# Differential attention in an 8-head, 1024-token layer: other banks and another order for projections, context weights and normalizing, and ScalarE in place of GpSimd for the high halves of copied parts

## The chip, the cores and the metric

The kernel runs on one core of a Trainium2 chip. A core has TensorE (PE in the profile; PEld are its weight loads), VectorE (DVE), ScalarE (ACT), GpSimd (POOL) and SyncE (SP), which here issues all transfers. Each engine works through its own list of instructions in order; semaphores hold an instruction until what it needs is there. PSUM, where TensorE puts its results, has eight banks of 512 fp32 columns. The metric is the device time of one execution in microseconds, the median of several. A single execution is also profiled, and all rows shown come from such an execution.

## The reference

Two layers over 1024 latent tokens and 256 context tokens of width 1024. Layer 0 mixes by differential attention and layer 1 by an S5 state-space layer; an MLP follows each. Only the attention of layer 0 is touched here:

```python
q_l = apply_rope(heads_qk(q_l), cos, sin) * scale      # 8 heads, 2 components of 64
k_l = apply_rope(heads_qk(k_l), cos, sin)
k_all = jnp.concatenate([k_c, k_l], axis=1)            # 256 context + 1024 latent keys
s = jnp.einsum('bqhcd,bkhcd->bhcqk', q, k)
p = jax.nn.softmax(s, axis=-1)
w = p[:, :, 0] - lam * p[:, :, 1]
o = jnp.einsum('bhqk,bkhe->bqhe', w, v)
o = rmsnorm(o, subln_g) * (1.0 - lambda_init)
```

Context queries see only context keys and have no rotary; latent queries see all 1280 keys. Everything is fp32.

## The kernel before

**Precision.** A product of two fp32 matrices is made of three matmuls (`mm3`, L132 to L134): each operand is split into a high half, which is a copy to fp32r (`split`, L137, on ScalarE), and a low half, the source minus the high half (L138, on VectorE or GpSimd).

**The stage.** Attention is the function `phase_b`. It goes through 8 heads with 9 units each, so 72 units `n`, and 5 more to finish. Unit 0 of a head holds the 256 context queries, units 1 to 8 hold 128 latent queries each. Queries are also counted in pairs of 256 (pair 0 is unit 0, pair 1 units 1 and 2, and so on). The loop writes the order of TensorE, VectorE, ScalarE and GpSimd out by hand (`manual`), and only SP's list is ordered by a scheduler.

A unit does the following, and the names are used from here on:

- *Scores* (L510, in unit 0 L504): two components, 2560 columns of PSUM, banks 0 to 4; in unit 0 banks 0 and 1 only.
- *Minima* (L523, L519 in unit 0): VectorE reads the scores (their sign is turned), writes them to SBUF and gathers the row minimum, once per component.
- *Exponentials* (L533, L530): ScalarE, one per component, with row sums.
- *Combination* (L541, L542, L544): VectorE makes the weights `w` of the unit.
- *Parts*: the weights of the unit before are transposed by TensorE (L556) in three parts of 4, 2 and 4 blocks of 128 columns, into bank 5, half of bank 6, and bank 7 or, if the unit has projection matmuls, bank 5 again. `w_evac` brings a part to SBUF as a high and a low half (`wT`). The first part goes directly: high on ScalarE (L564), low on VectorE (L565), both read PSUM. The others are *copied*: ScalarE copies the part to SBUF (L569), GpSimd makes high (L570) and low (L571) of the copy. Unit 0's weights have one part only, so unit 1 has one part to bring.
- *Values* (`values`): after each pair's second unit, in units 2 (pair 0, only 2 blocks), 4, 6, 8 and unit 1 of the next head, TensorE multiplies `wT` with the values into bank 6; they stand ahead of the transposes. In those units except for pair 0 the parts are brought to SBUF only after the combination. `pair_out` copies the result (L652), squares it on GpSimd (L653) and stores it to `od`.

**Projections of the next head.** Units 0, 2, 3, 5 and 7 make the queries and keys of head h+1 (`AHEAD`, `proj_group`): context keys and a first half of the latent keys in unit 0, the second half of the keys in unit 2, context queries in unit 3, the two halves of the latent queries in units 5 and 7. Every group is collected in bank 7 (the ring `qb`). The two groups of unit 0 differ: the first stands ahead of the scores and is brought out at once, the second is laid between the parts, as the groups of the other units are. A context group is brought out directly (L451, L452). A latent group goes through the rotary chain: `evac` at the end of its unit (L456, L457 and four transfers that swap rows), an empty step, `sine` on GpSimd (L462), `add` on VectorE (L465), `store` (a split, L137 and L138, and transfers to `Kd` or `Qd`). These steps lie in the list `post`; `next_post` takes one after the second part and one at the end of each unit. So the sine comes at the end of the next unit, the sum after the second part of the one after, and the store at its end.

**Normalizing of the head before.** In units 6, 7, 8, 0 and 1 one pair of the head before is normalized: `norm_load` at the start of the unit loads the pair from `od` and the factors from `rsd`; `norm_pair` at the end of the unit multiplies them (L684, VectorE), splits the product (high on ScalarE, L137 with 128x256 W<-W; low on GpSimd) and stores both to `on`. This starts in unit 6 of head 1, with head 0's result.

**Head 7** has no projections to make. In its units and the 5 that follow TensorE does the first part of the output projection (`wo_group`), and head 6's pairs are normalized by `norm6` and head 7's by `norm7`.

Of the kernel before, what the change touches and what calls it, by code (L numbers as in the profile page):

```python
# [70 lines left out]
class Prog:  # L71
# [359 lines left out]
    def proj_group(self, h, T, g, wt):  # L431
# [3 lines left out]
        b = self.qb.next()[:, 0:n]  # L435
# [35 lines left out]
        return [product(k) for k in range(8)], [direct] if g == 2 else [evac, None, sine, add, store]  # L471
# [89 lines left out]
    def w_evac(self, tb, hi, lo, direct):  # L561
        nc = self.nc
        if direct:
            nc.scalar.activation(hi, tb, AF.Copy)  # L564
            nc.vector.tensor_tensor(lo, tb, hi.bitcast(F32), ALU.subtract)  # L565
        else:
            m, n = tb.shape[1:]
            t = shaped(self.wraw.next()[:, 0 : m * n], (m, n))
            nc.scalar.activation(t, tb, AF.Copy)  # L569
            nc.gpsimd.tensor_scalar(hi, t, 1.0, 0.0, ALU.mult, ALU.add)  # L570
            nc.gpsimd.tensor_tensor(lo, t, hi.bitcast(F32), ALU.subtract)  # L571
# [8 lines left out]
    def b_start(self):  # L580
# [11 lines left out]
        for split, T in zip(splits, (1, 0)):  # L592
            split(0)
            wt = split(1)
            for g in (2, 0, 1):
                products, rest = self.proj_group(0, T, g, wt)
                for f in products:
                    f()
                for f in post:
                    f()  # L600
                rest[0]()
                post = rest[2:]
                yield
# [3 lines left out]
    def phase_b(self):  # L607
# [181 lines left out]
        ready = []  # L789
# [5 lines left out]
        with self.manual():  # L795
            for n in range(72 + 5):
# [6 lines left out]
                if front and n - 6 >= 9 and (n - 6) % 9 < 5 and (n - 6) // 9 < 7:  # L803
                    norm_load((n - 6) // 9 - 1, (n - 6) % 9)
                if h == 7 and u > 5:
                    load6(u)
                if front:
# [10 lines left out]
                    if h < 7:  # L818
                        groups = [self.proj_group(h + 1, *a, wts[a[0]]) for a in self.AHEAD.get(u, ())]
# [8 lines left out]
                    self.maxima(u, p, sm)  # L828
                if front:
# [12 lines left out]
                if pv:  # L842
                    values(*pv)
                for part in range(3):
                    if part < parts:
                        tb = pb[:, 256:512] if part == 1 else self.bank(7 if part == 2 and not groups else 5)
                        t = self.w_part(prev[1], prev[2], part, tb)
                        ready.append((*t, part == 0))
                    if not late or part == 2:
                        evac()  # L850
# [24 lines left out]
                next_post()  # L875
# [20 lines left out]
                if h < 8 and n - 6 >= 9 and (n - 6) % 9 < 5 and (n - 6) // 9 < 7:  # L896
                    norm_pair((n - 6) // 9 - 1, (n - 6) % 9)
# [1204 lines left out]
```

## Time and profile before

| | before |
|---|---|
| median of 3 runs | 3051.51 us (3049.69 to 3059.32) |
| profiled execution: time, span | 3048.01 us, 3046.2 us |
| granted clock of TensorE, mean | 0.978 |
| TensorE busy | 2855.1 us, 94% of the span |
| VectorE busy | 1909.6 us, 63% |
| ScalarE busy | 1256.1 us, 41% |
| GpSimd busy | 814.1 us, 27% |

The attention stage begins at about 238 us of the span and ends at about 905 us. In a row of a group of instructions the columns are: line, engine, operation, out<-in and shapes, count, then busy microseconds and mean nanoseconds of one, then the idle time of the engine just before them with what ended it. In a row in order of time they are: start, duration, engine, line, operation, and in brackets the idle time before it and what ended that. A row of waits has the total in microseconds, how often, and the longest.

### The profile page before, as it was taken

To read this page: it belongs to the slowest core of one execution; us is meant where nothing else is said; L and a number is where in the kernel's file an instruction comes from. 1 tells how busy PE (TensorE), PEld (TensorE's weight loads), DVE (VectorE), ACT (ScalarE), POOL (GpSimd) and SP (SyncE) were. 2 spreads that over 40 slices of the span, in tenths; PEclk is the share of its full clock that TensorE was granted. 3 is DMA by queue.
4 is the path that set the end of the run, shared out by engine and by line. 5 is a ranking of instruction groups with operands and counts; after the bars stand their busy time and mean duration, and the time that the engine had idled before them with its cause. 6 is when DMAs were issued, how large, how long until landed. Compare 5 with 4: busy or idle time off the path is not lost.

```text
span 3046.2 us, 42172 instructions
## 1 busy us (share of the span) xinstructions
PE 2855.1 (94%) x15376; PEld 2368.6 (78%) x15376; DVE 1909.6 (63%) x2766; ACT 1256.1 (41%) x2254; POOL 814.1 (27%) x794
## 2 busy tenths in 40 slices
PE   6998999999799999999999999688999899999998
PEld 4687888878687877788777778588787778888887
DVE  5357877777654654344677755899543666666555
ACT  3425555555544643333422222467344533222223
POOL 2314665666654400000100003566112200000003
PEclk9999999999899999999999999899999999999999
DMA  9955556556716455532666663577642221111113
GB/s 264 304 174 164 150 161 167 164 161 173 245 57 197 125 169 174 166 119 93 199 192 184 185 196 104 159 213 206 214 148 95 66 66 56 52 49 52 56 39 135
DMA packets 384235, 448.83 MB, mean 147 GB/s; under 512 B 54694, under 2 KB 299676, under 8 KB 382876
## 3 DMA queue, kind: packets, MB, share of 16 engines
q1 hardware_dynamic: 384028, 446.14, 49.1%
q8 instruction: 121, 1.98, 0.3%
q14 instruction: 86, 0.70, 0.1%
HBM read 320.88 MB, written 120.95 MB: 145 GB/s over the span
## 4 chain that ended last, share of the span: by engine, by line
PE 66%; DVE 10%; DMA 8%; issue 5%; ACT 4%; POOL 4%; SPq 3%; DVEq 0%; POOLq 0%; ACTq 0%
PE PS L132 19%; PE PS L134 19%; PE PS L133 19%; SPq L80 3%; PE PS L510 2%; ACT F L533 1%; PE PS L202 1%; DVE F L523 1%; DVE FD L1708 1%; PE PS L556 1%; PE PS L1690 1%; PE PS L1725 1%; DMA W<-rsd 1%; DVE FD L1699 1%; DVE R L138 1%
## 5 line engine op out<-in xcount | busy, mean ns | idle before, releaser
L132 PE MATMUL PS<-H,R 128*128 128x512 f32 (+1 forms) x960 | 361.3, 378 | 15.5 <-ACT F L569 13.8
L133 PE MATMUL PS<-H,R 128*128 128x512 f32 (+1 forms) x992 | 366.1, 369 | 2.9 <-POOL H L138 2.8
L134 PE MATMUL PS<-H,R 128*128 128x512 f32 (+1 forms) x960 | 348.9, 368 | 0.1
L133 PE MATMUL PS<-R,H 128*128 128x512 f32 x692 | 271.0, 392 | 0.0
L132 PE MATMUL PS<-R,H 128*128 128x512 f32 x676 | 268.2, 400 | 2.0 <-ACT R L137 1.6
L134 PE MATMUL PS<-R,H 128*128 128x512 f32 x676 | 260.1, 392 | 1.1 <-DVE H L138 1.1
L132 PE MATMUL PS<-R 128*128 128x256 f32 (+1 forms) x656 | 221.9, 339 | 7.0 <-ACT R L137 2.8
L132 PEld LDWEIGHTS PS<-H,R 128*128 128x128 f32 x960 | 184.3, 192 | 50.3 <-ACT F L569 15.2
L137 ACT ACTIVATE R<-W 128x512 fp32r<-128x512 f32 (+1 forms) x203 | 154.6, 766 | 161.1 <-PE PS L133 112.0
L1625 POOL TENSOR_SCALAR stat<-stat 128x1 f32<-128x1 f32 x24 | 14.9, 620 | 765.4 <-ACT PS L1623 765.1
L133 PE MATMUL PS<-R 128*128 128x256 f32 (+1 forms) x624 | 208.6, 334 | 9.1 <-DVE R L565 9.1
L1428 DVE TENSOR_TENSOR F<-PS,F 128x1024 f32<-128x1024 f32 (+1 forms) x113 | 136.4, 1212 | 128.3 <-PE PS L134 128.1
L133 PEld LDWEIGHTS PS<-H,R 128*128 128x128 f32 x992 | 191.4, 193 | 31.1 <-POOL H L138 3.6
L138 DVE TENSOR_TENSOR R<-W,R 128x512 fp32r<-128x512 f32 (+1 forms) x162 | 140.5, 872 | 114.5 <-ACT R L137 75.2
L134 PEld LDWEIGHTS PS<-H,R 128*128 128x128 f32 x960 | 184.3, 192 | 32.6 <-issue 2.1
L533 ACT ACTIVATE F<-F,stat 128x1280 f32<-128x1280 f32 x128 | 174.4, 1362 | 84.5 <-DVE F L523 84.2
L523 DVE TENSOR_SCALAR_CACHE_REDUCE F<-PS 128x1280 f32<-128x1280 f32 x128 | 185.1, 1483 | 8.6 <-PE PS L510 8.3
L570 POOL TENSOR_SCALAR R<-F 128x256 fp32r<-128x256 f32 (+1 forms) x128 | 124.2, 970 | 169.3 <-ACT F L569 147.5
L134 PE MATMUL PS<-R 128*128 128x512 f32 (+1 forms) x488 | 168.4, 354 | 0.0
L132 PE MATMUL PS<-H 128*128 128x512 f32 x408 | 161.0, 395 | 1.5 <-ACT H L137 1.5
L134 PE MATMUL PS<-H 128*128 128x512 f32 x408 | 159.4, 392 | 0.0
L510 PE MATMUL PS<-R,R 128*128 128x512 f32 x720 | 155.3, 364 | 0.4 <-DVE F L523 0.4
(426 smaller groups left out, 7037.8 us busy)
## 6 DMA issues: line engine op xcount, KB each, us to landing
W<-in_mlp_w SPq DMA_DIRECT2D x148, 256.0 KB
W<-in_mlp_w SPq DMA_DIRECT2D x68, 512.0 KB
FU<-in_ada_w SPq DMA_DIRECT2D x40, 512.0 KB
W<-in_ada_w SPq DMA_DIRECT2D x32, 512.0 KB
H<-hidd SPq DMA_DIRECT2D x64, 256.0 KB
W<-in_s_w_glu SPq DMA_DIRECT2D x64, 256.0 KB
hidd<-FU SPq DMA_DIRECT2D x52, 256.0 KB
recd<-FD SPq DMA_DIRECT2D x48, 256.0 KB
```

Of the source, the lines that this page charges most:

```text
L80: return self.nc.sync.dma_start(out=out, in_=in_)
L132: mm(out, ah, bh, start=first, stop=False, **kw)
L133: mm(out, ah, bl, start=False, stop=False, **kw)
L134: mm(out, al, bh, start=False, stop=last, **kw)
L137: self.nc.scalar.activation(hi, src, AF.Copy)
L138: (lo_eng or self.nc.vector).tensor_tensor(lo, src, hi.bitcast(F32), ALU.subtract)
L202: self.nc.tensor.matmul(acc[32 * j : 32 * j + 32, 0:256], self.scT[:, 2 * k : 2 * k + 32], w[:, 256 * j : 256 * j + 256], start=k == 0, st ...
L510: mm(self.PS[:, 1280 * c + k0 : 1280 * c + k1], Q[:, c, r, qs], K[c][:, k0:k1], start=r == 0, stop=r == 1)
L523: ts(p[c], self.PS[:, 1280 * c : 1280 * c + 1280], 1.0, None, ALU.mult, ALU.min, accum_out=sm[:, c : c + 1])
L533: nc.scalar.activation(p[c], p[c], AF.Exp, bias=sm[:, c : c + 1], scale=-1.0, accum_out=sn[:, 0:1] if c else s0[:, u + 1 : u + 2])
L570: nc.gpsimd.tensor_scalar(hi, t, 1.0, 0.0, ALU.mult, ALU.add)
L1428: nc.vector.tensor_tensor(acc[:, n : n + m], y[:, n : n + m], acc[:, n : n + m], ALU.add)
```

## The change

- The first of unit 0's two projection groups is collected in bank 4; all others stay in bank 7.
- The empty step of the rotary chain is dropped: the sine comes after the second part of the next unit, the sum one step later, the store after the second part of the unit after that.
- A new list `later` takes what used to be done at the end of a unit from `post`, and `norm_pair`. It is worked off in the next unit, right after the minima. `norm_load` comes behind it instead of at the unit's start.
- In units with values (except for pair 0) the first part is copied too, if the unit has three parts. If it has one (unit 1), its transposes stand ahead of the values, it goes directly, and it is brought out right away instead of after the combination.
- The high half of a copied part is made by ScalarE (still line L570) instead of GpSimd.

Units of all heads are affected alike; the stages before and behind are not edited.

```diff
-    def proj_group(self, h, T, g, wt):
+    def proj_group(self, h, T, g, wt, b=None):
...
-        b = self.qb.next()[:, 0:n]
+        b = (self.qb.next() if b is None else b)[:, 0:n]
...
-        return [product(k) for k in range(8)], [direct] if g == 2 else [evac, None, sine, add, store]
+        return [product(k) for k in range(8)], [direct] if g == 2 else [evac, sine, add, store]
...
             nc.scalar.activation(t, tb, AF.Copy)
-            nc.gpsimd.tensor_scalar(hi, t, 1.0, 0.0, ALU.mult, ALU.add)
+            nc.scalar.activation(hi, t, AF.Copy)
             nc.gpsimd.tensor_tensor(lo, t, hi.bitcast(F32), ALU.subtract)
...
-                post = rest[2:]
+                post = rest[1:]
...
-        ready = []
+        ready, later = [], []
...
-                if front and n - 6 >= 9 and (n - 6) % 9 < 5 and (n - 6) // 9 < 7:
-                    norm_load((n - 6) // 9 - 1, (n - 6) % 9)
...
-                        groups = [self.proj_group(h + 1, *a, wts[a[0]]) for a in self.AHEAD.get(u, ())]
+                        ahead = self.AHEAD.get(u, ())
+                        groups = [self.proj_group(h + 1, *a, wts[a[0]], self.bank(4) if a != ahead[-1] else None) for a in ahead]
...
                     self.maxima(u, p, sm)
+                while later:
+                    later.pop(0)()
+                if front and n - 6 >= 9 and (n - 6) % 9 < 5 and (n - 6) // 9 < 7:
+                    norm_load((n - 6) // 9 - 1, (n - 6) % 9)
...
-                if pv:
+                first = parts == 1
+                if pv and not first:
                     values(*pv)
                 for part in range(3):
                     if part < parts:
                         tb = pb[:, 256:512] if part == 1 else self.bank(7 if part == 2 and not groups else 5)
                         t = self.w_part(prev[1], prev[2], part, tb)
-                        ready.append((*t, part == 0))
-                    if not late or part == 2:
+                        ready.append((*t, part == 0 and (first or not late)))
+                    if pv and first and part == 0:
+                        values(*pv)
+                    if not late or first or part == 2:
                         evac()
...
-                next_post()
+                if post:
+                    later.append(post.pop(0))
...
                 if h < 8 and n - 6 >= 9 and (n - 6) % 9 < 5 and (n - 6) // 9 < 7:
-                    norm_pair((n - 6) // 9 - 1, (n - 6) % 9)
+                    later.append(lambda a=((n - 6) // 9 - 1, (n - 6) % 9): norm_pair(*a))
```

## The prediction

> **What bounds the kernel now.** I read the page first, then busy time by stage, the waits of the attention stage, and the order of time inside one head. The change touches only the attention stage, about 238 to 905 us of the span.
>
> ```profile
> span 3046.2 us, 42172 instructions
> PE 2855.1 (94%) x15376; PEld 2368.6 (78%) x15376; DVE 1909.6 (63%) x2766; ACT 1256.1 (41%) x2254; POOL 814.1 (27%) x794
> 238.00:905.00 667.00, 611.63 (x3763) 536.85 (x3763) 502.32 (x792) 374.19 (x743) 413.85 (x404) 0.97 0.55 159
> 551.25:555.90 4.65, 4.65 (x26) 4.65 (x27) 2.00 (x3) 0.64 (x2) 4.48 (x6) 0.63 0.78 220
> ...
> 551.25 0.39 PE L132 MATMUL PS<-H,R 128*128 128x256 f32 x1 [2.54 <-ACT F L569]
> ```
>
> The third row is the stage (columns after the length: busy time of TensorE, its weight loads, VectorE, ScalarE and POOL, each with its instructions, then the granted clock); the last two are used further down. In the stage TensorE is busy 612 of 667 us, VectorE (DVE) 502, GpSimd (POOL) 414, ScalarE (ACT) 374. No engine is full, so the question is which loop of waits sets the pace. The waits of the stage, and one head in order of time:
>
> ```profile
> ACT F L533 <- DVE F L523: 84.2, 53, 4.5
> DVE stat L541 <- ACT F L533: 73.4, 58, 2.4
> DVE W L684 <- DMA W<-rsd: 34.0, 16, 4.6
> PE PS L556 <- DVE R L565: 20.3, 14, 2.9
> PE PS L132 <- ACT F L569: 13.8, 6, 2.6
> PE PS L133 <- DVE R L565: 9.1, 6, 2.4
> ...
> 526.76 1.49 DVE L523 TENSOR_SCALAR_CACHE_REDUCE F<-PS 128x1280 f32<-128x1280 f32 x1 [0.20 <-PE PS L510]
> 528.17 1.49 DVE L523 TENSOR_SCALAR_CACHE_REDUCE F<-PS 128x1280 f32<-128x1280 f32 x1
> 528.29 1.37 ACT L533 ACTIVATE F<-F,stat 128x1280 f32<-128x1280 f32 x1 [2.31 <-DVE F L523]
> 529.70 1.36 ACT L533 ACTIVATE F<-F,stat 128x1280 f32<-128x1280 f32 x1
> 531.65 1.55 DVE L544 SCALAR_TENSOR_TENSOR F<-F,stat 128x1280 f32<-128x1280 f32 x1
> 533.92 0.64 DVE L684 SCALAR_TENSOR_TENSOR W<-W,lamc 128x256 f32<-128x256 f32 x1
> 534.49 1.48 DVE L523 TENSOR_SCALAR_CACHE_REDUCE F<-PS 128x1280 f32<-128x1280 f32 x1
> 545.57 1.48 DVE L523 TENSOR_SCALAR_CACHE_REDUCE F<-PS 128x1280 f32<-128x1280 f32 x1
> 556.68 0.41 DVE L519 TENSOR_SCALAR_CACHE_REDUCE F<-PS 128x256 f32<-128x256 f32 x1
> 566.78 1.48 DVE L523 TENSOR_SCALAR_CACHE_REDUCE F<-PS 128x1280 f32<-128x1280 f32 x1
> 577.33 1.49 DVE L523 TENSOR_SCALAR_CACHE_REDUCE F<-PS 128x1280 f32<-128x1280 f32 x1
> 585.69 1.48 DVE L523 TENSOR_SCALAR_CACHE_REDUCE F<-PS 128x1280 f32<-128x1280 f32 x1
> 594.13 1.48 DVE L523 TENSOR_SCALAR_CACHE_REDUCE F<-PS 128x1280 f32<-128x1280 f32 x1
> 602.10 1.48 DVE L523 TENSOR_SCALAR_CACHE_REDUCE F<-PS 128x1280 f32<-128x1280 f32 x1
> 610.06 1.49 DVE L523 TENSOR_SCALAR_CACHE_REDUCE F<-PS 128x1280 f32<-128x1280 f32 x1 [0.18 <-PE PS L510]
> ```
>
> VectorE and ScalarE wait for each other in every unit (84.2 and 73.4 us). The rows of unit 6 show the loop: row minima at 526.76, first exponential 1.53 later, second 1.41 after that, combination at 531.65, ending at 533.20. That is 6.44 from minima to the end of the combination, 3.50 of it after the second exponential starts. What stands on VectorE between that end and the next minima is paid in full; what stands between minima and combination falls into the 1.5 us in which VectorE waits anyway, provided ScalarE isn't held up. The first minima of units 6, 7, 8, 0, 1, 2, 3, 4, 5, 6 are the rows from 526.76 to 610.06: intervals 7.73, 11.08, 11.11, 10.10, 10.55, 8.36, 8.44, 7.97, 7.96, together 83.3 us a head. So I sum the change over these intervals and not over TensorE.
>
> **The change, part by part.** Durations are means of the stage, so what the engines take from each other is in them:
>
> ```profile
> L684 DVE SCALAR_TENSOR_TENSOR W<-W,lamc 128x256 f32<-128x256 f32 x30 | 23.6, 787 | 36.6 <-DMA W<-rsd 34.0 <-DMA W<-od 2.5
> L465 DVE TENSOR_TENSOR FC<-FC 128x512 f32<-128x512 f32 x28 | 27.8, 993 | 2.3 <-POOL FC L462 2.3
> L138 DVE TENSOR_TENSOR R<-FC,R 128x512 fp32r<-128x512 f32 x28 | 29.8, 1064 | 10.4 <-ACT R L137 10.4
> L457 DVE SCALAR_TENSOR_TENSOR FC<-PS,W 128x512 f32<-128x512 f32 x28 | 19.4, 692 | 6.9 <-ACT FC L456 4.4
> L565 DVE TENSOR_TENSOR R<-PS,R 128x512 fp32r<-128x512 f32 x72 | 49.3, 684 | 3.4 <-ACT R L564 3.4
> L452 DVE SCALAR_TENSOR_TENSOR R<-PS,R 128x256 fp32r<-128x256 f32 x13 | 5.5, 421 | 6.8 <-ACT R L451 6.8
> L564 ACT ACTIVATE R<-PS 128x512 fp32r<-128x512 f32 x72 | 42.5, 590 | 45.5 <-PE PS L556 42.7 <-PE PS L551 2.1
> L569 ACT ACTIVATE F<-PS 128x512 f32<-128x512 f32 x64 | 38.1, 596 | 22.2 <-POOL R L571 7.0 <-PE PS L556 5.8 <-POOL R L138 4.6
> L569 ACT ACTIVATE F<-PS 128x256 f32<-128x256 f32 x64 | 23.9, 374 | 8.1 <-PE PS L556 7.7
> L137 ACT ACTIVATE R<-FC 128x512 fp32r<-128x512 f32 x28 | 17.9, 639 | 5.0 <-DMA Kd<-R 5.0
> L137 ACT ACTIVATE W<-W 128x256 fp32r<-128x256 f32 x30 | 12.5, 418 | 96.6 <-DVE W L684 43.5 <-POOL R L571 29.9 <-POOL R L138 8.9
> L652 ACT ACTIVATE FC<-PS 128x256 f32<-128x256 f32 x39 | 15.2, 389 | 0.0
> L570 POOL TENSOR_SCALAR R<-F 128x512 fp32r<-128x512 f32 x63 | 77.5, 1230 | 24.9 <-ACT FC L660 21.1 <-ACT F L569 3.8
> L570 POOL TENSOR_SCALAR R<-F 128x256 fp32r<-128x256 f32 x64 | 46.0, 719 | 143.7 <-ACT F L569 143.7
> ```
>
> 1. High halves on ScalarE. POOL loses the L570 groups (123.5 us) and gains 24 low halves of first parts (some 30 us at L570's 1.23, the nearest row here); both lie beside the loop. ScalarE gains 152 copies from SBUF to SBUF, one per copied part; no such row exists for these tiles, the nearest is L137: 0.64 for 512 columns, 0.42 for 256, which I take. In units without values one such 256 copy now stands between the two exponentials: +0.42 on the loop. In units with values the copies come after both exponentials; the first part becomes a copy too (L565, 0.68, leaves the gap behind the combination in units 4, 6 and 8), but ScalarE then has 0.60+0.63+0.37+0.42+0.60+0.63 = 3.25 us of copies in a row before the next unit's work.
>
> 2. Normalizing moved. L684 and its ScalarE high half leave the end of a unit and come after the next unit's minima; the load follows them and has a whole unit to land, so I take the 34.0 us of waits for it as gone. But the high half (L137, 0.42) is queued on ScalarE ahead of L564 and of the first exponential, and it waits for both minima, for the rotary sum L465 where there is one (units 7, 0, 2), and for L684. So the first exponential starts not 1.53 but 2.82+0.99+0.79+0.42+0.59 = 5.6 us after the minima in units 7 and 2, 4.0 in unit 8, 4.6 in unit 1.
>
> 3. The rotary chain one step earlier. The store's low half (L138, 1.06) leaves the gap; its high half (L137, 0.64) now stands between the exponentials in units 2, 4, 7 and 0, and in unit 4 it waits for the sum.
>
> 4. Bank 4 for the first of two groups at unit 0. It removes the wait for bank 7 (the 13.8 row, 6 times, 2.3 us a head) and the slow clock behind it (0.63 in the row 551.25: 4.65 x 0.37 = 1.7 us). What is late next: the group's evacuation on ScalarE is behind unit 8's copies, and the next minima are behind that evacuation.
>
> 5. Transposes ahead of values in unit 1, so the first part's low half is made before the combination: the 9.1 row goes. The values after it then wait for the pair's copy to od (L652), which is behind both exponentials; I take 0 for the two together. SP issues the same transfers; where its order changed, I price it at 0, since each store and load has about a unit of slack, with the 34.0 us as the cost if not.
>
> The sum, interval by interval, after against before:
> - Unit 6: between 6.44 and 7.73, middle 7.1: -0.6.
> - Unit 7: 5.62, exponential 1.41, copy 0.37, high copy 0.42, store 0.64, then 3.50 and L457 0.69: 12.65 against 11.08: +1.6.
> - Unit 8: 2.82+0.79+0.42, two exponentials 2.82, copies 3.25, L652 0.39, the group's evacuation (0.39 on ScalarE, taken as L652, and L452, 0.42): 11.3 against 11.11: +0.2.
> - Unit 0: the wait for the Kd store (5.0 us in 5) goes, normalizing and copies come before the exponentials: 0, plus or minus 1.
> - Unit 1: 4.62+1.41+3.50 = 9.5 against 10.55: -1.0.
> - Unit 2: as unit 7, 12.65 against 8.36: +4.3. Here normalizing arrives that stood in unit 1 before.
> - Unit 3: +0.4 (high copy). Unit 4: 2.82+0.99+0.64+3.50 = 7.95 against 7.97: 0. Unit 5: high copy, and the copies of unit 4 still on ScalarE: +0.4.
>
> That is +5.3 a head. POOL now has less with which to hold VectorE up; with L465 and L684 at the pace of L565 (0.68 and half of it) units 7, 2, 8 and 1 are 0.75, 0.75, 0.45 and 0.45 shorter: +2.9. I take +4.3. It holds for the five passes from unit 6 of a head to unit 5 of the next in heads 1 to 6: +21. Heads 0 and half of 1 normalize nothing: six stores at -0.4 and four L565 at -0.7 against eight high copies at +0.4: -2. From unit 6 of head 6 on no projections follow and the DMA waits were longest (4.6 the longest one): I estimate -7, from two or three such waits against the later exponentials. Sum: +12.
>
> The profiled execution took 3048.0 us (span 3046.2), the median of the runs is 3051.5; +12 on the median gives 3063.
>
> **Two rules of the skill against these rows.** The granted clock fell to 0.63 right behind an idle stretch of 2.54 us on TensorE (the 13.8 row's kind). The Trainium skill, "TensorE: Matmul & The Clock Gate", section "What's actually happening", has the clock halved only after about 3.4 us without work; by that rule the stalls of 2 to 3 us that I expect would cost no clock. The row says otherwise, and that is the third rival below.
> The Trainium skill, "SBUF — State Buffer", section "Who interferes with whom", says that a VectorE instruction with two SBUF inputs and a GpSimd instruction that reads SBUF exclude each other for the whole instruction. By that rule fewer POOL instructions shorten L138, L465 and L684; it speaks for the first rival.
>
> **The rivals.**
> - Faster: TensorE's waits, not the loop, set the pace. Then the three PE rows (20.3+13.8+9.1 = 43 us) and the slow clock go, and L138, L465 and L684 lose what POOL costs them: 81 us in sum against 48 at L565's pace, an estimate. Half of 43 plus a few us of this is -25: 3026. For it: the 34.0 us of DMA waits surely shrink, POOL loses 123.5 us. Against it: the order on ScalarE, where the exponentials stand behind normalizing. It decides if the intervals of units 7 and 2 stay below about 10 us on average. Chance 0.25.
> - No change: the later exponentials cost +2.9 a head or less, and the two ends give it back: within 0.3% (9 us, about what can be told apart here). Chance 0.28.
> - Slower by the clock as well: the new stalls of TensorE in units 0, 2 and 5 (its transposes wait for the later combinations) pull the clock as the 2.54 us did; two a head in five heads at 1.7 us is +17 more: 3080. Chance 0.12.
> - Slower since the load still lands late: half of the 34.0 us back: 3080. Chance 0.05.
> - The forecast itself, 0.30. Together faster 0.25, same 0.28, slower 0.47. Range 3032 to 3088; the forecast's own 3061 to 3075.
>
> **What would show it.** Right: the first exponential starts 4 us or more after the minima in units 7, 8, 1, 2; intervals of units 7 and 2 near 12.5; no wait L684 for W<-rsd; no wait of L132 for L569 at unit 0; ScalarE's busy time up by about 80 us; no L570 on POOL. Wrong: if units 7 and 2 come out at 10 or less, VectorE's own instructions became shorter than I took, and the forecast's sign falls.

## The result, and the profile after

The changed kernel takes 3065.38 us (median, 3058.55 to 3070.74) where the kernel before, timed beside it, takes 3049.69 (3042.13 to 3059.42). The ratio is 1.0049, with a 95% interval of 1.0034 to 1.0063: slower by about 15 us. The forecast was 3063, in a range of 3032 to 3088. In the profiled executions the span went from 3046.2 to 3066.0, by 19.8 us: the one after ran somewhat longer than its median, the one before somewhat shorter.

The first fence is the head of the page of the changed kernel; the second the row of the attention stage, with the same columns as before (length; busy time of TensorE, weight loads, VectorE, ScalarE, POOL; granted clock, DMA share, GB/s).

```profile
span 3066.0 us, 42391 instructions
PE 2869.4 (94%) x15376; PEld 2370.5 (77%) x15376; DVE 1885.1 (61%) x2742; ACT 1327.3 (43%) x2406; POOL 745.0 (24%) x690
```

```profile
238.00:905.00 667.00, 603.92 (x3646) 523.33 (x3645) 464.18 (x748) 430.87 (x866) 332.65 (x287) 0.96 0.54 157
```

ScalarE has 152 instructions and 71 us more over the whole kernel, VectorE 24 instructions and 24 us less, POOL 104 instructions and 69 us less. In the same 667 us, though, TensorE got 117 matmuls fewer done: the stage ends some 20 us later. In these 667 us three engines were busy for less time and one for longer, and that does not say why. The waits of the stage, taken from 238 to 925 us since it ends later, do (engine, tile and line that waits, what it waits for: us in total, times, longest).

```profile
DVE stat L541 <- ACT F L533: 103.7, 64, 3.5
DVE W L684 <- DMA W<-od: 2.5, 1, 2.5
ACT F L533 <- DVE F L523: 55.9, 23, 4.2
PE PS L556 <- DVE F L544: 30.7, 19, 2.8
```

The load wait of L684 went as forecast: 34.0 us of `W<-rsd` before, one wait of 2.5 for `W<-od` now. The wait of the exponentials for the minima fell from 84.2 to 55.9, because something else now stands in front of them; VectorE's wait for the exponentials rose from 73.4 to 103.7, and TensorE's wait for the combination L544, 30.7 us here, was one of 1.4 us before. Unit 7 of head 4 in order of time (start, length):

```profile
630.65 1.49 DVE L523 TENSOR_SCALAR_CACHE_REDUCE F<-PS 128x1280 f32<-128x1280 f32 x1 [0.56 <-PE PS L510]
632.07 1.49 DVE L523 TENSOR_SCALAR_CACHE_REDUCE F<-PS 128x1280 f32<-128x1280 f32 x1
633.48 0.95 DVE L465 TENSOR_TENSOR FC<-FC 128x512 f32<-128x512 f32 x1
634.35 1.51 DVE L684 SCALAR_TENSOR_TENSOR W<-W,lamc 128x256 f32<-128x256 f32 x1
635.89 0.42 ACT L137 ACTIVATE W<-W 128x256 fp32r<-128x256 f32 x1 [3.31 <-DVE W L684]
636.22 0.58 ACT L564 ACTIVATE R<-PS 128x512 fp32r<-128x512 f32 x1
636.70 1.35 ACT L533 ACTIVATE F<-F,stat 128x1280 f32<-128x1280 f32 x1
...
638.77 0.61 ACT L137 ACTIVATE R<-FC 128x512 fp32r<-128x512 f32 x1
639.29 1.35 ACT L533 ACTIVATE F<-F,stat 128x1280 f32<-128x1280 f32 x1
...
641.21 1.55 DVE L544 SCALAR_TENSOR_TENSOR F<-F,stat 128x1280 f32<-128x1280 f32 x1
...
643.28 1.48 DVE L523 TENSOR_SCALAR_CACHE_REDUCE F<-PS 128x1280 f32<-128x1280 f32 x1
```

The same stretch as a row of the stage, for the granted clock (1.00):

```profile
630.65:643.28 12.63, 11.09 (x59) 8.90 (x58) 9.23 (x12) 8.88 (x18) 7.67 (x8) 1.00 0.30 81
```

The first minima were done by 632.14, and with that the first exponential could have started. It starts at 636.70, because ScalarE takes its instructions in order and the high half of the normalized pair (635.89) is queued ahead of it; that waits for L684, which waits for both minima and the rotary sum. ScalarE idles 3.31 us with work at hand. The unit takes 12.63 us from minima to minima. A slower TensorE is not the reason: its clock stood at 1.00 in unit 7 of all five passes of the table below, and unit 2 takes 11.42 us in heads 2 to 6, whether the clock fell in it (heads 3 and 6) or not.

Interval from minima to minima in us, worked out from the starts of the first L523 (L519 in unit 0) of each unit; "3/4" is unit 6 of head 3 to unit 5 of head 4, and so on. The column "forecast" is the prediction's list before its correction from +5.3 to +4.3 a head. The last column is the experiment e2 below.

| unit | before 3/4 | forecast | after 3/4 | after 4/5 | e2 3/4 |
|---|---|---|---|---|---|
| 6 | 7.73 | 7.1 | 7.09 | 7.01 | 8.45 |
| 7 | 11.08 | 12.65 | 11.92 | 12.63 | 9.72 |
| 8 | 11.11 | 11.3 | 10.42 | 10.42 | 9.71 |
| 0 | 10.10 | 10.1 | 12.52 | 9.71 | 10.62 |
| 1 | 10.55 | 9.5 | 9.22 | 9.20 | 8.93 |
| 2 | 8.36 | 12.65 | 11.42 | 11.42 | 8.17 |
| 3 | 8.44 | 8.8 | 8.86 | 8.87 | 9.11 |
| 4 | 7.97 | 8.0 | 7.52 | 7.52 | 7.52 |
| 5 | 7.96 | 8.4 | 10.65 | 10.61 | 10.60 |

Over the five passes from unit 6 of one head to unit 5 of the next the changed kernel loses 5.6, 0.6, 6.3, 4.4 and 3.4 us, together 20.3. (Unit 0 in the column "after 3/4" is the longest of its kind; in heads 2, 3, 5 and 6 it takes 9.2 to 10.1 us.)

### The profile page after: what moved, and what is told of

Its sections match the earlier page's. It is cut to its first block, busy times and chain, and to the rows that moved or that the text cites. A ratio compares the mean times of both kernels' runs of the same rounds, so it can differ in the third digit from the quotient of the medians.

```text
span 3066.0 us, 42391 instructions
## 1 busy us (share of the span) xinstructions
PE 2869.4 (94%) x15376; PEld 2370.5 (77%) x15376; DVE 1885.1 (61%) x2742; ACT 1327.3 (43%) x2406; POOL 745.0 (24%) x690
## 4 chain that ended last, share of the span: by engine, by line
PE 51%; DVE 7%; DMA 4%; POOL 4%; issue 3%; ACT 3%; SPq 2%; DVEq 0%; POOLq 0%; ACTq 0%
PE PS L132 16%; PE PS L134 15%; PE PS L133 15%; SPq L80 2%; PE PS L202 1%; DVE FD L1715 1%; PE PS L1697 1%; PE PS L1732 1%; DVE FD L1706 1%; DMA H<-hidd 1%; POOL FD L1677 1%; DVE FD L1613 1%; DVE H L138 0%; DMA W<-in_mlp_w 0%; PE PS L510 0%
## 5 line engine op out<-in xcount | busy, mean ns | idle before, releaser
L132 PE MATMUL PS<-H,R 128*128 128x512 f32 (+1 forms) x960 | 362.7, 380 | 1.7 <-ACT R L137 1.1
L132 PE MATMUL PS<-R,H 128*128 128x512 f32 x676 | 269.2, 401 | 1.7 <-ACT R L137 1.6
L571 POOL TENSOR_TENSOR R<-F,R 128x512 fp32r<-128x512 f32 (+1 forms) x152 | 194.0, 1288 | 201.2 <-ACT R L570 131.9
L132 PE MATMUL PS<-R 128*128 128x256 f32 (+1 forms) x656 | 222.3, 340 | 9.7 <-ACT FC L652 4.3
L138 DVE TENSOR_TENSOR R<-W,R 128x512 fp32r<-128x512 f32 (+1 forms) x162 | 140.5, 872 | 117.9 <-ACT R L137 76.7
L132 PEld LDWEIGHTS PS<-H,R 128*128 128x128 f32 x960 | 184.1, 192 | 36.1 <-issue 5.4
L533 ACT ACTIVATE F<-F,stat 128x1280 f32<-128x1280 f32 x128 | 173.5, 1356 | 56.1 <-DVE F L523 55.9
L523 DVE TENSOR_SCALAR_CACHE_REDUCE F<-PS 128x1280 f32<-128x1280 f32 x128 | 185.4, 1485 | 11.2 <-PE PS L510 10.7
L132 PE MATMUL PS<-H 128*128 128x512 f32 x408 | 161.3, 395 | 1.2 <-ACT H L137 1.2
```

What stands on the lines that cost most here:

```text
L132: mm(out, ah, bh, start=first, stop=False, **kw)
L138: (lo_eng or self.nc.vector).tensor_tensor(lo, src, hi.bitcast(F32), ALU.subtract)
L523: ts(p[c], self.PS[:, 1280 * c : 1280 * c + 1280], 1.0, None, ALU.mult, ALU.min, accum_out=sm[:, c : c + 1])
L533: nc.scalar.activation(p[c], p[c], AF.Exp, bias=sm[:, c : c + 1], scale=-1.0, accum_out=sn[:, 0:1] if c else s0[:, u + 1 : u + 2])
```

## The experiments

The theory: the normalizing of a pair, moved between a unit's minima and its exponentials, is what makes the kernel slower. Rivals: the high halves on ScalarE do it; the earlier rotary chain does it (the sum L465 shares that gap); or each part is a loss or a gain of its own and they add up. The ratios below stand against the kernel before, timed beside each experiment; a difference of two ratios, times 3050, gives the us between two experiments.

**e2: the changed kernel, only the normalizing put back.**

```
+                if front and n - 6 >= 9 and ...:          # at the unit's start
+                    norm_load((n - 6) // 9 - 1, (n - 6) % 9)
...
-                if front and n - 6 >= 9 and ...:          # behind the minima
-                    norm_load((n - 6) // 9 - 1, (n - 6) % 9)
...
-                    later.append(lambda a=((n - 6) // 9 - 1, (n - 6) % 9): norm_pair(*a))
+                    norm_pair((n - 6) // 9 - 1, (n - 6) % 9)
```

> As the changed kernel, but normalizing is where it was before the change: load at the start of a unit, product and split at its end. Theory: the exponentials start on time again (-2.5 to -4 us in units 7, 8, 0, 1, 2), while L684 and its waits for W<-rsd come back (2 us a unit on average): -6 to -9 us a head, 3020 to 3035 us, so that the other parts of the change alone beat the kernel before. Rival 1 (high halves on ScalarE): within 5 us of the changed kernel. Rival 3 (moving normalizing is itself the gain of the change and something else loses): slower than the changed kernel by 10 us or more.

Measured: 3035.29 us, ratio 0.9959 (0.9945 to 0.9974), at the upper end of what the theory expected. So the rest of the change is a gain of about 13 us, and moving the normalizing turns it into a loss: 27 us lie between the two. The waits and the start of unit 7 of head 4:

```profile
DVE stat L541 <- ACT F L533: 86.0, 64, 3.5
DVE W L684 <- DMA W<-rsd: 27.0, 17, 2.6
```

```profile
619.31 1.48 DVE L523 TENSOR_SCALAR_CACHE_REDUCE F<-PS 128x1280 f32<-128x1280 f32 x1
620.83 1.37 ACT L533 ACTIVATE F<-F,stat 128x1280 f32<-128x1280 f32 x1 [0.38 <-DVE F L523]
628.32 1.48 DVE L523 TENSOR_SCALAR_CACHE_REDUCE F<-PS 128x1280 f32<-128x1280 f32 x1
```

The exponential is back at 1.52 us behind the minima and the unit takes 9.01 instead of 12.63. The load waits that the move had removed are back too, 27.0 us, and yet the kernel is 27 us faster. Not all of that need be the exponentials: summed over the stage, the granted clock fell short of full speed by 25.6 us in the changed kernel and by 13.9 here (an estimate from windows of 1 us), so up to 12 us can be the clock's. In units 7 and 2, where most of the difference lies, it is not.

**e5: the kernel before, only the normalizing moved** (`later`, its loop behind the minima and the load behind it, as in the change; nothing else).

> The kernel before with one edit: the normalizing of a pair (load, product L684, split) moved behind the next unit's minima, as the change has it; rotary chain, banks, order and high halves stay those of the kernel before. Theory (the normalizing in the gap before the first exponential is the loss, 2.5 to 3 us in each of five units of a head, whatever else is there): slower than before by 20 to 45 us, 3070 to 3095, with the first exponential of units 7, 8, 0, 1, 2 at 3.5 us or more after the minima, and the waits of L684 for W<-rsd gone. Rival (the loss comes only where the rotary sum and the normalizing share the gap, and by itself the move just gives back its load waits): within 10 us of before, 3040 to 3060.

Measured: 3067.9 us, ratio 1.0056 (1.0036 to 1.0076): +17 us. The rival falls; the theory's range, 3070 to 3095, began a little too high. The first exponential starts 4.2 us behind the minima in units 7 and 2, 3.7 in units 8 and 1, and 2.7 in unit 0 (expected were 3.5 or more). Here the waits of the stage are

```profile
ACT W L137 <- DVE W L684: 79.7, 19, 7.9
DVE stat L541 <- ACT F L533: 107.0, 63, 3.2
```

In head 4 units 7, 8 and 2 go from 11.07, 10.89 and 8.36 to 12.42, 13.11 and 11.08, against 0.5 to 1.5 us won in each of units 6, 0 and 1. So the loss comes without the rotary sum in the gap, and it is the same ScalarE queue: 79.7 us in which the high half at its head waits for L684. In the kernel before that wait was 43.5 us, at the ends of units, where no exponential stood behind it. Part of unit 8's loss is the clock's, which falls for twice as long there as before in most heads (3.4 against 1.7 us short); units 7 and 2 are longer by 1.4 and 2.6 us in head 2 too, where the clock stayed at 1.00 in both.

**e1: the changed kernel, with only the product L684 behind the minima; the split and the next load come behind the second exponential.**

```
-        def norm_pair(h, pair):
+        def norm_product():
             nc.vector.scalar_tensor_tensor(nob, nob, self.sg, nrb, ALU.mult, ALU.mult)
+
+        def norm_split(h, pair):
             self.split(nhi, nlo, nob, nc.gpsimd)
...
+                    if part == 1:
+                        for f in todo_halves:
+                            f()
+                        if front and n - 6 >= 9 and ...:
+                            norm_load((n - 6) // 9 - 1, (n - 6) % 9)
```

> As the changed kernel, but only the product L684 stays right after the minima; the split of the product (high half on ScalarE, low half on GpSimd) and the next load come after the second exponential. Theory (the high half of the normalized pair, queued ahead of the exponentials, makes the loop of VectorE and ScalarE longer): the first exponential is back at 1.5 to 2 us after the minima, units 7, 8, 0, 1, 2 lose 2 to 3.5 us each until TensorE's own work bounds them (9.4, 9.9, 8.0, 6.4 and 9.7 us), about -9 us a head in five heads: near 3020 us, below both kernels. Rival 1 (the high halves of copied parts on ScalarE are what costs): no more than -5 us in all. Rival 2 (slow clock behind new stalls of TensorE): unit 5 stays at 10.6 and the gain is half, near 3043 us.

Measured: 3054.79 us, ratio 1.002 (1.0009 to 1.0031). Better than the changed kernel, but a miss against 3020. The exponentials start 1.5 us behind the minima again (2.3 in unit 7), and units 7 and 8 took 9.8 and 9.2 us, where 9.4 and 9.9 were expected. What the edit broke is the load: it goes out behind the split of the pair before, whose low half stands in GpSimd's queue behind the sine product L462, and that had waited 5.17 us for a transfer of its own. The waits of the stage, and unit 2 of head 4:

```profile
DVE W L684 <- DMA W<-od: 35.6, 18, 5.0
```

```profile
578.08 0.46 SPq L80 DMA_DIRECT2D W<-od  x1
...
582.18 0.48 DVE L684 SCALAR_TENSOR_TENSOR W<-W,lamc 128x256 f32<-128x256 f32 x1 [3.29 <-DMA W<-od]
584.50 1.55 DVE L544 SCALAR_TENSOR_TENSOR F<-F,stat 128x1280 f32<-128x1280 f32 x1
```

The load is issued at 578.08, and VectorE stands until 582.18 with the combination behind it: unit 2 takes 11.86 us (8.17 in e2; 11.2 to 16.1 in heads 2 to 6 of e1). A late load at the end of a unit delays the next minima; the same late load between minima and combination delays the combination and then the minima.

**e3: the changed kernel, high halves on GpSimd again.**

```
-            nc.scalar.activation(hi, t, AF.Copy)
+            nc.gpsimd.tensor_scalar(hi, t, 1.0, 0.0, ALU.mult, ALU.add)
```

> As the changed kernel, but the high halves of copied parts are made by GpSimd again. Theory: the second exponential comes 0.4 us earlier in units 0, 2, 3, 5, 7, and ScalarE has 1.7 us less behind the exponentials of units 4, 6, 8; against it VectorE's L138, L465, L684 get slower again by what GpSimd takes: -2 to +1 us a head, 3055 to 3070 us. Rival 1: -3 us a head or more, back to 3050 us or less.

Measured: 3068.44 us, ratio 1.0067 (1.005 to 1.0084), which is not to be told from the changed kernel's 1.0049. The high halves are not what makes the change slow. With the normalizing where the change has it, they gain some 5 us, not told from nothing.

**e4: the changed kernel, rotary chain as before.**

```
-        return [product(k) for k in range(8)], [direct] if g == 2 else [evac, sine, add, store]
+        return [product(k) for k in range(8)], [direct] if g == 2 else [evac, None, sine, add, store]
...
-                if post:
-                    later.append(post.pop(0))
+                next_post()
```

> As the changed kernel, but the rotary chain has its empty step again and its last step stands at the end of a unit, as before the change. Theory: the store's low half (L138, 1.06 us) goes back behind the combination in four units, its high half (0.64 us) leaves the space between the exponentials, and the sum no longer stands ahead of normalizing in units 7, 0 and 2 (0.7 to 1 us each): about -1 us a head, 3055 to 3068 us. If moving the chain was the loss: below 3050 us.

Measured: 3090.91 us, ratio 1.0142 (1.0127 to 1.0157): 28 us slower than the changed kernel, where 3055 to 3068 us had been expected. In this kernel the earlier chain is a large gain, where the expectation, made with the prediction's durations, had it at a loss of 1 us a head. Unit 2 of head 4:

```profile
599.75 0.48 DVE L684 SCALAR_TENSOR_TENSOR W<-W,lamc 128x256 f32<-128x256 f32 x1 [2.33 <-DMA W<-od]
601.12 1.35 ACT L533 ACTIVATE F<-F,stat 128x1280 f32<-128x1280 f32 x1
...
605.12 1.55 DVE L544 SCALAR_TENSOR_TENSOR F<-F,stat 128x1280 f32<-128x1280 f32 x1
606.67 1.70 DVE L138 TENSOR_TENSOR R<-FC,R 128x512 fp32r<-128x512 f32 x1
```

The store's low half L138 (1.70 us) stands in the gap behind the combination, where all of it is paid, and the load of the normalizing comes late besides: L684 waits 2.33 us for it, with both exponentials behind. The unit takes 14.57 us (11.42 in the changed kernel). How the 28 us divide between the two was not measured by itself; e7, with the normalizing at the end of the unit, still has 23.

**e6, e7, e9, e10: the changed kernel with the normalizing put back (e2), and one more part put back in each**: bank 4 (e6), the rotary chain (e7, e4's edit), the order and the copies of the context weights (e9), the high halves (e10, e3's edit). The edits of e6 and e9:

```
-  groups = [self.proj_group(h + 1, *a, wts[a[0]], self.bank(4) if a != ahead[-1] else None) for a in ahead]
+  groups = [self.proj_group(h + 1, *a, wts[a[0]], None) for a in ahead]
```

```
-                if pv and not first:
+                if pv:
                     values(*pv)
...
-                        ready.append((*t, part == 0 and (first or not late)))
-                    if pv and first and part == 0:
-                        values(*pv)
-                    if not late or first or part == 2:
+                        ready.append((*t, part == 0))
+                    if not late or part == 2:
```

> The changed kernel with the normalizing put back as in e2_norm_back, and bank 4 put back too: the first of the two projection groups of unit 0 takes a bank of the ring again. Against e2_norm_back (3035). Theory: the wait of 2.3 us for bank 7 and the slow clock behind it return at six heads, but the minima of unit 0 waited for the direct copy anyway, so bank 4 is worth 0 to 10 us: 3035 to 3045. Rival (bank 4 is a main source of the gain of e2): 3048 or more.

> The changed kernel with the normalizing put back as in e2_norm_back, and the rotary chain put back too (its empty step again, its last step at the end of a unit). Against e2_norm_back (3035). Theory (the earlier chain is a gain by itself, since e4_chain_back lost 25 against the changed kernel): 3048 to 3062. Rival (the chain put back was dear in e4 only because its tail met the moved normalizing): 3033 to 3045.

> The changed kernel with the normalizing put back as in e2_norm_back, and the order and copies of the context weights put back too: values ahead of the transposes in unit 1, and part 0 of the units with values written straight from the bank (one VectorE subtraction more, one ScalarE copy fewer) instead of copied. Against e2_norm_back (3035). Theory (these edits are near nothing, as predicted for the order): 3030 to 3042. Rival (they hold the 20 us by which the change without its normalizing falls short of what the chain, 28, and bank 4, 6, are worth by e7 and e6): 3012 to 3025. If they are a gain of their own: 3045 or more.

> The changed kernel with the normalizing put back as in e2_norm_back, and the high halves of the copied parts made by GpSimd again. Against e2_norm_back (3035). Theory (as in e3_high_pool, 3 us worse): 3033 to 3045. Rival (the high halves on ScalarE hold the missing 20 us, since ScalarE's copies stand ahead of its second exponential once the normalizing is out of the way): 3012 to 3025.

**e12: the kernel before, only the high halves on ScalarE.**

> The kernel before with one edit: the high halves of the copied parts of the context weights made by ScalarE (L570) instead of GpSimd. Theory (this part pays only together with the earlier rotary chain and the other order: e7_norm_chain, which has it without the earlier chain, is 14 slower than before, although e10_norm_pool shows it worth 20 with the chain early): 3050 to 3070. Rival (it is a gain of its own of 10 to 20 us that adds to the others): 3030 to 3040.

Measured, with what each says of its part (minus is a gain):

| kernel | time, us | ratio (interval) | the part | it does |
|---|---|---|---|---|
| e6 | 3040.94 | 0.9977 (0.9964 to 0.9991) | bank 4, beside the rest without normalizing | -5 (intervals overlap) |
| e7 | 3063.11 | 1.0036 (1.0023 to 1.0048) | chain earlier, the same way | -23 |
| e9 | 3052.68 | 1.0009 (0.9997 to 1.002) | order and copies, the same way | -15 |
| e10 | 3055.52 | 1.0016 (1.0006 to 1.0025) | high halves on ScalarE, the same way | -17 |
| e12 | 3068.14 | 1.0054 (1.0037 to 1.0072) | high halves on ScalarE, alone on the kernel before | +16 |

The four parts together gain 13 us (e2); taking away any one of them takes away between 5 and 23, together some 60. So they don't add up. The one part of the four that was tried alone on the kernel before is a loss there: +16 for the high halves, with the chain late. That part's sign depends on the others; e3 adds that its 17 us shrink to some 5, not told from nothing, when the normalizing is moved. The other three were not tried alone. For e6 and e12 the theory held, and for e7 to within some 1 us; of e9 and e10 the rival (that they hide a loss of 20) and the theory (near nothing) both fell, and for e9 the third case named there, a gain of its own, came true.

Why the high halves need the early chain, in unit 2 of head 5 of e12:

```profile
676.51 1.55 DVE L544 SCALAR_TENSOR_TENSOR F<-F,stat 128x1280 f32<-128x1280 f32 x1
677.25 1.97 POOL L571 TENSOR_TENSOR R<-F,R 128x512 fp32r<-128x512 f32 x1 [1.58 <-ACT FC L660]
...
678.06 1.71 DVE L138 TENSOR_TENSOR R<-FC,R 128x512 fp32r<-128x512 f32 x1
679.88 0.69 DVE L457 SCALAR_TENSOR_TENSOR FC<-PS,W 128x512 f32<-128x512 f32 x1
680.49 1.48 DVE L523 TENSOR_SCALAR_CACHE_REDUCE F<-PS 128x1280 f32<-128x1280 f32 x1
```

The unit's minima started at 670.98. In the kernel before, in unit 2 of head 4, the combination starts 5.07 us behind the minima (577.33 to 582.40); here it is 5.53, since a high half of 0.42 stands between the exponentials. There L138 took 1.10, here 1.71. That is 0.46 + 0.61 = 1.07 of the 1.15 us by which the unit is longer (9.51 against 8.36). Units 3 and 4 are longer too, by 1.2 and 0.8 us. Over the stage the store's low half takes, in e12 and in the changed kernel:

```profile
L138 DVE TENSOR_TENSOR R<-FC,R 128x512 fp32r<-128x512 f32 x28 | 40.5, 1447 | 12.5 <-ACT R L137 12.5
L138 DVE TENSOR_TENSOR R<-FC,R 128x512 fp32r<-128x512 f32 x28 | 22.5, 803 | 39.0 <-ACT R L137 33.3 <-DMA on<-W 3.8 <-DMA W<-od 1.9
```

With the chain late its mean is 1.06 us (before) and 1.25 (e5) while GpSimd makes the high halves, and 1.45 (e12), 1.50 (e7) and 1.62 (e4) when ScalarE makes them. With the chain early it is below 1 us in every kernel (0.72 to 0.96), and L138 no longer stands in the gap behind the combination.

Why they pay once the chain is early, in unit 7 of head 4 of e10, where GpSimd makes them again:

```profile
629.02 1.19 POOL L138 TENSOR_TENSOR W<-W 128x256 fp32r<-128x256 f32 x1
631.69 1.31 SPq L80 DMA_DIRECT2D W<-od  x1
635.07 0.95 DVE L684 SCALAR_TENSOR_TENSOR W<-W,lamc 128x256 f32<-128x256 f32 x1 [2.55 <-DMA W<-od]
635.95 1.48 DVE L523 TENSOR_SCALAR_CACHE_REDUCE F<-PS 128x1280 f32<-128x1280 f32 x1
```

GpSimd comes to the normalized pair's low half at 629.02, 5.3 us behind the minima (623.68; in e2 3.0 us), so its input comes free later, the next load is issued later (631.69), and the next minima wait for it: the unit takes 12.27 us where e2 has 9.01. The longer copies on ScalarE buy an earlier GpSimd, and the earlier GpSimd an earlier load. e10 is not e12 turned round: its GpSimd also has the high halves of the first parts that are copied since the change, and order and bank differ. That the early chain alone turns the sign is therefore argued from these rows and not shown by a run. What e9's 15 us are made of no single wait shows: unit 4 takes 8.1 to 9.1 us instead of 7.5, unit 5 takes 10.3 to 10.6 in heads 1 to 6 where e2 has three such heads, and the rest is spread over many units.

**e8: e2, and the 256-column group of unit 0 written out through the idle rotary buffer.**

```
+        if own:                                        # set for that group alone
+            s = shaped(self.rq, (2, 256)).bitcast(F32R)
```

> The changed kernel with the normalizing put back as in e2_norm_back, and the direct group of unit 0 (256 columns) written out through the idle rotary buffer in place of the staging buffer that the following store needs. In e2_norm_back ScalarE's L137 of that store waits 4.6 us for the write of Kd at unit 0, with both second exponentials behind it, and five such waits sum to 18.8 us. Theory: that wait goes and unit 0 falls by 3 to 5 us in heads 1 to 6: 3010 to 3025. Rival (the values or the next unit's scores end unit 0 anyway): 3030 to 3037.

Measured: 3033.28 us, ratio 0.9942 (0.9922 to 0.9963), not to be told from e2. Its waits (lines are two further down than elsewhere: L459 is L457):

```profile
DVE R L138 <- ACT R L137: 12.8, 17, 1.7
DVE FC L459 <- ACT FC L458: 19.0, 19, 4.2
```

L138's wait fell from 30.1 us to 12.8, and unit 0 became 9.5 us shorter over heads 1 to 6. But the wait of the rotary product for its ScalarE copy rose from 10.2 to 19.0, 7.5 us of it because the buffer is still being written out to Kd when the next group wants it, and other units became longer. Most of the gain was given back. The time lies in the rival's range, but not for its reason, since unit 0 did become shorter.

**e11: e8, and each next load of the normalizing issued right behind the product**, which writes the low half's buffer in place of its own input. The first load of a head stays at the start of unit 6.

```
...
         def norm_pair(h, pair):
-            nc.vector.scalar_tensor_tensor(nob, nob, self.sg, nrb, ALU.mult, ALU.mult)
-            self.split(nhi, nlo, nob, nc.gpsimd)
+            t = nlo.bitcast(F32)
+            nc.vector.scalar_tensor_tensor(t, nob, self.sg, nrb, ALU.mult, ALU.mult)
+            if pair < 4:
+                norm_load(h, pair + 1)
+            self.split(nhi, nlo, t, nc.gpsimd)
```

> e8_norm_stage (3033) with the next pair's load issued right behind the product: the product L684 writes the low half's buffer in place of its own input, so the input is free one GpSimd step sooner and the load goes out ahead of the two writes of the halves. In e8 L684 waits 27.6 us in 16 places for W<-rsd, with the next unit's minima behind it. Theory: those waits go but for the first of each head, and half of that reaches the end: 3012 to 3026. Rival (the minima then wait for their scores, which PE ends at the same time): 3028 to 3036.

Measured: 3026.75 us, ratio 0.9927 (0.9907 to 0.9947): faster than the kernel before by some 22 us, and the lowest median of all. It falls between what theory and rival had expected, and its interval overlaps that of e8. The waits for the load (L687 is L684):

```profile
DVE W L687 <- DMA W<-rsd: 7.6, 6, 1.7
DVE W L687 <- DMA on<-W: 6.8, 7, 2.8
```

27.6 us became 7.6, and 6.8 for the write of the halves came in. This is the version that gets what the move was to bring (a load that has landed) without a place on ScalarE's queue in front of the exponentials. What the early load itself is worth in time, 6.5 us against e8, is not told from nothing.

## Why the prediction was right, and where it was not

The forecast was 3063 and the time 3065, and the mechanism is the one forecast: the exponentials start late behind the normalizing, and units 7 and 2 pay for it. That the number came out within 2 us is in part luck. The forecast was +12 on a median that came out 2 us lower in the later runs; the medians differ by 15, the two profiled executions by 19.8, and in these the terms for the two ends of the stage miss by 10 us together. By the prediction's steps:

- Step 2, normalizing: right. First exponential 6.1 us behind the minima in unit 7 (5.6 forecast), 3.7 in unit 8 (4.0), 4.2 in unit 1 (4.6), 4.8 in unit 2 (5.6); unit 8 thus misses the 4 us that the prediction had named as a sign. Unit 7 came to 12.6 as forecast, but with L684 at 1.51 us where 0.79 was taken; unit 2 came to 11.4 and unit 8 to 10.4 where 12.65 and 11.3 were forecast, as L465 and L684 take less there (0.68 and 0.47 in unit 2 of head 4). e2 and e5 show this step to be the loss: +17 alone, +27 on top of the rest.
- Step 1, high halves: "+0.42 on the loop" is near what the traces show in the changed kernel itself, where units 7 and 2 are 0.6 and 0.5 us shorter in e3. What the step left out shows in the other kernels: what the copies do to L138 in the gap when the chain is late (e12: +16 in all), and that GpSimd's time decides when the next load goes out (e10: 17 lost).
- Step 3, the chain: the prediction gives it no sum of its own, and e4's expectation, from the same durations, was -1 us a head for putting it back. It measured 28 us the other way. The duration that failed is 1.06 for L138, which is 1.62 in e4; the late load in unit 2 comes on top.
- Step 4, bank 4: the wait of L132 for L569 went, and the next minima wait for the group's evacuation as said. Worth some 5 us, and not told from none.
- Step 5, order in unit 1: the 9.1 us row went, L132 waits 4.3 us for L652 in its place. e9 shows order and copies together to be worth 15 beside the rest, where 0 was taken for the order.
- The sum by place: +20.3 in the five passes, where +21 was forecast; +1.5 at the start (from unit 0 of head 0 to unit 6 of head 1), where -2 was; -0.5 from unit 6 of head 6 to unit 8 of head 7, where -7 was. The passes hide two errors that cancel in the column "after 4/5": units 2 and 8 together 2.1 lower than forecast, unit 5 2.2 higher. At the start it is unit 5 again, 1.0 and 1.1 longer in heads 0 and 1. The end is the term that was mis-sized most. Its premise, that no projections follow from unit 6 of head 6 on, is not so: unit 7 still makes the last queries of head 7, and the rotary sums stand ahead of the normalizing in unit 7 (2.2 us longer) and in unit 0 of head 7. Unit 6 gained 5.0 as the load wait there went, but unit 1 of head 7 lost 4.5:

```profile
837.35 1.49 DVE L523 TENSOR_SCALAR_CACHE_REDUCE F<-PS 128x1280 f32<-128x1280 f32 x1 [0.19 <-PE PS L510]
...
839.29 0.39 SPq L80 DMA_DIRECT2D on<-W  x1
839.73 0.42 SPq L80 DMA_DIRECT2D W<-od  x1
...
842.89 0.48 DVE L684 SCALAR_TENSOR_TENSOR W<-W,lamc 128x256 f32<-128x256 f32 x1 [2.53 <-DMA W<-od]
843.46 0.42 ACT L137 ACTIVATE W<-W 128x256 fp32r<-128x256 f32 x1 [5.95 <-DVE W L684]
844.26 1.35 ACT L533 ACTIVATE F<-F,stat 128x1280 f32<-128x1280 f32 x1
```

Here the load is issued only at 839.73, behind the write of the pair before, and with the product in front of the exponentials the late load delays these to 6.9 us behind the minima. That is the rival "the load still lands late", in one unit.

The rival "slower by the clock as well" came true in part. Unit 5 takes 10.4 to 10.6 us in four of the heads 1 to 6, where 8.4 was forecast. TensorE waits there for unit 4's combination, which the forecast for unit 5 left out, and its clock falls behind that wait; in two heads the same wait leaves the clock at 1.00, and the unit takes 9.05. Head 4, then head 3:

```profile
613.22 1.09 PE L556 MATMUL PS<-ident,F 128*128 128x128 f32 x4 [2.49 <-DVE F L544]
525.20 0.63 PE L556 MATMUL PS<-ident,F 128*128 128x128 f32 x4 [2.48 <-DVE F L544]
```

```profile
613.00:622.00 9.00, 8.78 (x40) 7.25 (x40) 5.40 (x9) 6.66 (x13) 6.62 (x7) 0.81 0.33 103
525.00:534.00 9.00, 8.80 (x48) 7.43 (x49) 6.34 (x10) 7.28 (x15) 8.22 (x7) 1.00 0.35 104
```

At a granted clock of 0.81 the transposes of the second part come late, ScalarE waits 1.53 us for them, and with it the second exponential. So of the 2.6 us by which unit 5 is longer than before, some 1.1 come without the clock and some 1.5 with it. Over the stage the clock fell short by 25.6 us after and 17.7 before (an estimate from windows of 1 us), so it can hold at most 8 of the 20 us; the rival had priced it at 17. e2 (24.3 us of L556 waiting for L544) and e11 (22.8) have the same wait, so it does not come from the normalizing.

## What to carry to other kernels

An instruction that gets out of a busy engine's way by moving earlier must be followed through every queue that it enters: here VectorE had room behind the minima, but the ScalarE copy that came with it stood in front of the exponentials and waited for all of VectorE's work there. If the aim is an earlier load, the load's buffer can be freed earlier and the work left where it is: that cut the load waits from 27.6 to 7.6 us (e11), though the time by no more than the noise. Parts of a change can be worth 17 us with the others and cost 16 without, so a part's price is measured in the company in which it will run.

## What the runs showed of the hardware

- In the changed kernel TensorE stalls at the start of unit 5 in each of heads 1 to 6, for 2.33, 2.81, 2.48, 2.49, 2.53 and 2.51 us. Behind the second, fourth, fifth and sixth the granted clock fell; after the 2.49 us of head 4 it was 0.60, 0.50, 0.50 and 0.69 in the four us from 613 on and 0.81 over 9 us (the row above), about 1.7 us short in sum. Behind 2.33 and 2.48 it stayed at 1.00. So the length of the stall does not decide it alone, and what does was not tested. The Trainium skill, "TensorE: Matmul & The Clock Gate", section "What's actually happening", has the clock fall after an idle window of about 3.4 us; by that rule none of these stalls would have cost anything. The trace does not agree: here a shorter stall was enough in four cases of six, as one of 2.54 us was in the kernel before.
- In the fence of e12 POOL's L571 (1.97 us; 1.29 with VectorE out of its way, as in e10) starts while L544 runs, and L138 (1.71 us; 0.68 otherwise) starts while L571 runs. From the end of L544 (678.06) to that of L571 (679.22) are 1.16 us, and from there to the end of L138 (679.77) 0.55, each 0.13 less than the instruction takes undisturbed: the three ran about one after the other. The Trainium skill, "SBUF — State Buffer", section "Who interferes with whom", says that a VectorE instruction with two inputs in SBUF and a GpSimd instruction that reads SBUF contend for a shared pair of ports that one holds at a time; these rows agree. So a low half on GpSimd lengthened VectorE's gap by a microsecond though GpSimd itself was on nobody's path. This was read from rows; no run took GpSimd's instruction away there. The means of L138 further up, 1.45 to 1.62 us in three kernels against 1.06 and 1.25 in two, go the same way.
